# A hybrid attention and GLA layer on one core: the 256-token chunk moved from fifth place to first

## The chip, the cores and the metric

The kernel runs on one core of a Trainium2 chip. The metric is the device time of one launch in microseconds (us), the median of several runs. The engines are TensorE (PE in the profile, PEld for its weight loads), VectorE (DVE), ScalarE (ACT), GpSimd (POOL) and SyncE (SP, which issues most DMAs). Each engine works through its own instructions in order; semaphores make one wait for another.

## What is computed

One layer of a decoder, on 2048 prompt tokens and 64 sample tokens (8 sequences of 8), model width 1024, in float32. Cut to what matters here:

```python
z = jnp.einsum('btd,dn->btn', x, w_in)
q, k, v, g_att, gq, gk, gv, g_gla, g_lr, r_att, r_gla = jnp.split(z, SPLIT_POINTS, axis=-1)
o_att = swa_prompt(q, k, v, attn_sink, rel_table)      # blocks of 128 queries on 256 keys
log_a = jax.nn.log_sigmoid(g_lr @ w_gk_up + b_gk) / 16.
o_gla, S = gla(gq * HK**-0.5, gk, gv, log_a, s0)       # chunked recurrence, state S per head
h_att = (o_att * silu(g_att)) @ w_pa
h_gla = (norm(o_gla) * silu(g_gla)) @ w_pg
merged = sigmoid(r_att) * h_att + sigmoid(r_gla) * h_gla
x = layer_norm(DN_ALPHA * x + merged @ w_o, ln_g, ln_b)
```

The samples go through the same layer with a cache of 128 keys and values and an incoming GLA state. The outputs are the two new x, the last keys and values, and the GLA states.

## The kernel before

**Numbers.** A float32 matrix product is done as three fp32r matmuls: each operand is split into a high part (ACT casts it, line 115) and the rest (line 116, on DVE, in some places on POOL), and high x high, low x high and high x low are summed in PSUM. `proj` (line 176) does this for one output tile: eight slices of 128 inputs, three matmuls each, 24 in all.

**Phases.** Attention (lines 551 to 656), GLA (lines 892 to 972), then the merge of both branches (lines 1115 to 1243) and the output projection with layer norm. Attention and GLA work in chunks of tokens, whose starts and lengths stand in `CHUNKS` (line 42). Attention runs over the chunks once; in each it makes the steps k, v, q0 to q3, a narrow one for the GLA decay (`gl`, lines 637 to 639) and ga0 to ga3. GLA runs over the four heads and in each head over all chunks: one narrow matmul for the decay (`gla_z`, line 686), then v in pieces of 128 tokens (`proj_t`, lines 198 to 200), k, q and two gates. The last chunk, 320 long, is 256 prompt tokens and the 64 samples.

**Weights.** In attention's first chunk each step takes a weight of 512 KB (`wt1`, `wload`): SP loads it into one of two staging buffers (`wst`), ACT casts it, DVE makes the low half (lines 130 to 134). Later chunks use the same ten weights. The first weight comes in four quarters, between the eight pieces of the first chunk's x (lines 229 to 235). During attention's last chunk six GLA weights are loaded, one per step.

**x.** The next chunk's x is fetched in eight pieces and split while the present chunk's gates run (`fetch_x`, `part_x`). There are 20 buffers for 16 parts, so only two pieces can be split ahead; each of the others waits for a slice of the last gate step to be used up.

**Order.** PE's order is the order of the code. Work that hangs on a step's result, such as scores, transposes and outputs, is put in a list of due times, `at(d, fn)`, and one entry is issued after every step (`tick`). A block of 128 queries in attention is issued like this, where `o` is 1 + 3 * bi, 2 more in the first chunk, counted from the last q step:

```python
at(o, lambda A=A, bi=bi: att_scores(A, bi, 0))
at(o + 1, lambda A=A, bi=bi: att_scores(A, bi, 1))
at(o + 3, lambda A=A, bi=bi: att_trans(A, bi, 0))
at(o + 4, lambda A=A, bi=bi: att_trans(A, bi, 1))
at(o + (6 if last and bi else 5), lambda A=A, bi=bi: att_out(A, bi))
```

Five steps follow in the same chunk, so blocks 1 and 2 are finished during the next chunk. `att_scores` (line 367) adds the bias to the scores from PSUM (L384, DVE), takes the maximum (L387, DVE), the exponentials (L390, L392, ACT) and scales (L396, DVE). `att_trans` (line 399) transposes the result on PE (L406) and copies it out as pT, one half on ACT (L410), one on DVE (L408). `att_out` (line 413) multiplies by v (L421) and gates (L424, DVE). In GLA `chain` (line 870) does the same with blocks of the recurrence; a 256-token chunk other than the last has its own due times there (`short`). The samples' state updates (L840) belong to the last chunk and are issued during the next head's first.

The instruction order on ACT, DVE, POOL and SP is set by a scheduler when the kernel is built, from its own estimates. The relative bias table of attention is made during the first chunk (`setup0` to `setup3`): eight tiles in PSUM (L301, L302), copied out by ACT (L306) and DVE (L304). Five PSUM buffers serve all this side work (`pa`), three the steps (`pd`).

Of the kernel before, what the change touches and what calls it, by code (L numbers as in the profile page):

```python
# [38 lines left out]
HV = 256  # L39
CH = 64  # L40

CHUNKS = [(0, 384), (384, 384), (768, 384), (1152, 384), (1536, 256), (1792, 320)]
TM = 384
MT = 352
MS = NT // (2 * MT)
# [6 lines left out]
def kernel(ctx, tc, io):  # L52
# [61 lines left out]
    def split(dst_h, dst_l, src, eng=nc.vector):  # L114
        pin["a"] = nc.scalar.copy(dst_h, src)  # L115
        i = eng.tensor_tensor(dst_l, src, dst_h.bitcast(F32), ALU.subtract)  # L116
        if eng is nc.vector:
            pin["d"] = i
# [5 lines left out]
    def wload(n=1):  # L124
        for _ in range(n):
            i = wseq[0]
            if i >= wseq[1]:
                return
            wseq[0] += 1
            st = sb.tile([P, D], F32, tag="wst", name="wst", bufs=2)  # L130
            pin["w"] = nc.sync.dma_start(st, io["wt"][i])
            hi = wtile(F32R, "wh")
            lo = wtile(F32R, "wl")
            split(hi, lo, st)
            wready.append((hi, lo))
# [12 lines left out]
    def fetch(src, k, t0, T, stage=xstage):  # L148
        st = stage()
        nc.sync.dma_start(st[:, :T], src[:, k, t0:t0 + T])  # L150
        return st, T

    def part(f, new=xnew, eng=nc.vector, samples=False):
        st, T = f
        hi, lo = new(), new()
        split(hi[:, :T], lo[:, :T], st[:, :T], eng)
        if samples:
            nc.gpsimd.tensor_copy(hi[:, T:T + NS], lo[:, T - NS:T])
        return hi, lo
# [4 lines left out]
    def fetch_x(src, t0, T):  # L164

        return [fetch(src, k, t0, T, unit if k < KT // 2 else xstage) for k in range(KT)]
# [63 lines left out]
    for k in range(KT):  # L230
        if k % 2 == 0:
            cs = slice(k * P, (k + 2) * P)
            nc.sync.dma_start(st[:, cs], io["wt"][0, :, cs])
            split(hi[:, cs], lo[:, cs], st[:, cs])
        x.append(part(fetch(io["xT"], k, *CHUNKS[0], unit)))
    wload(2)
# [296 lines left out]
    def wcap(n):  # L533
        wseq[1] = n
# [3 lines left out]
    def gate_in(h, c):  # L538

        t0, T = CHUNKS[c]  # L540
        if c == 0:
# [10 lines left out]
    kprev = vprev = None  # L552
    for c, (t0, T) in enumerate(CHUNKS):
        last = c == len(CHUNKS) - 1
        Tp = T - (NS if last else 0)
# [89 lines left out]
        for g in range(G):  # L645
# [3 lines left out]
            if g == 1:  # L649
                with tc.issue_after(pin["w"].ins) if c == 0 else nullcontext():  # L650
                    xf = fetch_x(io["xT"], *CHUNKS[(c + 1) % len(CHUNKS)])
            if g == G - 2:
# [239 lines left out]
    for h in range(GH):  # L892
        W2 = {}
        wcap(16 + 6 * h)
        for c, (t0, T) in enumerate(CHUNKS):
            last = c == len(CHUNKS) - 1
# [542 lines left out]
```

## Time and profile before

| | us |
|---|---|
| median of 3 runs (lowest, highest) | 1846.34 (1845.18, 1847.78) |
| the profiled execution, its own time | 1846.22 |
| its span | 1844.4 |
| PE busy | 1807.9 |
| DVE busy | 1280.9 |
| ACT busy | 849.9 |
| POOL busy | 422.3 |
| attention, first matmul to the start of GLA | 4.89 to 353.86 |
| GLA, to the last head's last chunk | 353.86 to 1061 |

Times in the rows are counted from the span's start. "Busy" of PE is made of modelled ends of pipelined matmuls, so the distance between the starts of two matmuls says more than the duration of one. "Idle before" names the time in which an engine had nothing to do just before an instruction, and what ended it. The granted clock is 1.00 at 2.4 GHz and 0.50 at 1.2 GHz.

### The profile page before, as it was taken

What the parts mean: (1) busy time and instruction counts of PE and PEld (TensorE: products, weight loads), DVE (VectorE), ACT (ScalarE), POOL (GpSimd) and SP (SyncE); (2) the same over time, 40 slices, a digit from 0 to 9 for tenths busy, and PEclk for the clock granted to TensorE, in tenths of its full rate; (3) what the DMA queues carried; (4) which work ended last, traced back from release to release, by engine and by line L of the source; (5) the groups of instructions that cost most, each with busy time, mean ns of one, the idle gap of its engine ahead of it and who ended that gap; (6) DMA issues with size and microseconds to landing.
All of it is one profiled execution on the core that took longest, in us unless ns stands there. A gap on an engine that the chain in (4) does not pass through costs nothing.

```text
span 1844.4 us, 32399 instructions
## 1 busy us (share of the span) xinstructions
PE 1807.9 (98%) x11683; PEld 1722.2 (93%) x11683; DVE 1280.9 (69%) x2662; ACT 849.9 (46%) x1947; POOL 422.3 (23%) x559
## 2 busy tenths in 40 slices
PE   8999999999999999999999999999999999989997
PEld 7998988899999999999999999999999999988886
DVE  5677778767776776777667669648657566966655
ACT  5444545645665565656546453435443543211110
POOL 3310111300110111011110243430355153631111
PEclk9999999999999999999999999999999999999998
DMA  7211013534345444543543189858887967895531
GB/s 233 63 56 38 12 47 100 165 131 156 120 148 170 143 143 144 186 132 107 181 145 119 58 274 315 283 178 292 276 311 256 310 216 245 287 312 177 166 111 41
DMA packets 199554, 315.84 MB, mean 171 GB/s; under 512 B 21453, under 2 KB 161189, under 8 KB 199376
## 3 DMA queue, kind: packets, MB, share of 16 engines
q1 hardware_dynamic: 192624, 304.61, 50.5%
q0 software_dynamic: 5616, 7.58, 1.5%
q8 instruction: 92, 1.51, 0.3%
q10 hardware_dynamic: 1152, 1.57, 0.3%
q14 instruction: 70, 0.57, 0.1%
HBM read 228.52 MB, written 86.14 MB: 171 GB/s over the span
## 4 chain that ended last, share of the span: by engine, by line
PE 91%; DVE 3%; DMA 3%; issue 1%; POOL 1%; SPq 0%; ACT 0%; DVEq 0%; ACTq 0%; POOLq 0%
PE pd L185 11%; PE pd L187 11%; PE pd L186 11%; PE pa L1234 9%; PE pa L1233 9%; PE pa L1232 9%; PE pd L199 7%; PE pd L198 7%; PE pd L200 7%; PE pa L421 2%; DMA cs<-tt_d 1%; PE pa L406 1%; PE pa L755 1%; PE pa L753 1%; PE pa L754 1%
## 5 line engine op out<-in xcount | busy, mean ns | idle before, releaser
L185 PE MATMUL pd<-x,wh 128*128 128x384 f32 (+2 forms) x1248 | 409.1, 328 | 7.0 <-ACT x L115 6.3
L186 PE MATMUL pd<-x,wh 128*128 128x384 f32 (+2 forms) x1248 | 403.5, 323 | 0.6 <-DVE x L116 0.3
L187 PE MATMUL pd<-x,wl 128*128 128x384 f32 (+2 forms) x1248 | 403.1, 323 | 0.6 <-DVE wl L116 0.6
L1233 PE MATMUL pa<-xl,wh 128*128 128x352 f32 x1176 | 381.3, 324 | 7.9 <-DVE xl L116 7.6
L1232 PE MATMUL pa<-xh,wh 128*128 128x352 f32 x1176 | 381.4, 324 | 2.6 <-ACT xh L115 2.3
L1234 PE MATMUL pa<-xh,wl 128*128 128x352 f32 x1176 | 381.9, 325 | 0.0
L185 PEld LDWEIGHTS pd<-x,wh 128*128 128x128 f32 x1248 | 236.5, 190 | 17.2 <-issue 8.9
L186 PEld LDWEIGHTS pd<-x,wh 128*128 128x128 f32 x1248 | 236.5, 190 | 2.0 <-DVE x L116 1.5
L187 PEld LDWEIGHTS pd<-x,wl 128*128 128x128 f32 x1248 | 236.1, 189 | 1.0 <-DVE wl L116 1.0
L1233 PEld LDWEIGHTS pa<-xl,wh 128*128 128x128 f32 x1176 | 222.7, 189 | 10.4 <-DVE xl L116 10.1
L1232 PEld LDWEIGHTS pa<-xh,wh 128*128 128x128 f32 x1176 | 222.5, 189 | 3.6 <-ACT xh L115 2.6
L1234 PEld LDWEIGHTS pa<-xh,wl 128*128 128x128 f32 x1176 | 224.5, 191 | 0.0
L116 DVE TENSOR_TENSOR xl<-xs,xh 128x1408 fp32r<-128x1408 f32 x63 | 110.5, 1753 | 69.4 <-ACT xh L115 35.7
L198 PE MATMUL pd<-wh,x 128*128 128x256 f32 x512 | 147.9, 289 | 0.0
L199 PE MATMUL pd<-wh,x 128*128 128x256 f32 x512 | 145.6, 284 | 1.2 <-DVE x L116 1.1
L200 PE MATMUL pd<-wl,x 128*128 128x256 f32 x512 | 144.6, 282 | 0.0
L115 ACT CAST x<-xst 128x384 fp32r<-128x384 f32 (+2 forms) x164 | 78.2, 485 | 139.9 <-PE pd L199 117.9
L115 ACT CAST xh<-xs 128x1408 fp32r<-128x1408 f32 x63 | 86.5, 1372 | 103.9 <-PE pa L1234 81.7
L746 POOL TENSOR_SCALAR sq<-sq 128x1 f32<-128x1 f32 (+1 forms) x68 | 21.4, 314 | 467.2 <-ACT ring L745 467.2
L199 PE MATMUL pd<-woh,x 128*128 128x512 f32 x256 | 101.5, 396 | 0.0
L198 PE MATMUL pd<-woh,x 128*128 128x512 f32 x256 | 101.5, 396 | 0.0
L200 PE MATMUL pd<-wol,x 128*128 128x512 f32 x256 | 101.5, 396 | 0.0
(318 smaller groups left out, 3683.6 us busy)
## 6 DMA issues: line engine op xcount, KB each, us to landing
wst<-wt SPq DMA_DIRECT2D x33, 512.0 KB, 3.6
xs<-xc_d SPq DMA_DIRECT2D x24, 704.0 KB, 5.6
cs<-tt_d SPq DMA_DIRECT2D x48, 352.0 KB, 4.7
u<-xT SPq DMA_DIRECT2D x84, 192.0 KB, 4.0
xst<-xT SPq DMA_DIRECT2D x76, 192.0 KB, 2.6
xs<-xT SPq DMA_DIRECT2D x18, 704.0 KB, 5.9
ws<-w_ra SPq DMA_DIRECT2D x36, 256.0 KB, 4.4
ws<-w_rg SPq DMA_DIRECT2D x36, 256.0 KB, 5.6
```

Source lines behind the costliest of these rows:

```text
L115: pin["a"] = nc.scalar.copy(dst_h, src)
L116: i = eng.tensor_tensor(dst_l, src, dst_h.bitcast(F32), ALU.subtract)
L185: mm(ps, hi[:, s], xh[:, :T], start=(k == 0), stop=False)
L186: mm(ps, hi[:, s], xl[:, :T], start=False, stop=False)
L187: mm(ps, lo[:, s], xh[:, :T], start=False, stop=(k == n - 1))
L198: mm(ps, xh[:, xs], hi, start=(k == 0), stop=False)
L199: mm(ps, xl[:, xs], hi, start=False, stop=False)
L200: mm(ps, xh[:, xs], lo, start=False, stop=(k == KT - 1))
L421: mm(ot[pr, :], vb[:, pr], A["pT", bi, kv][:, hf], start=(hf == h0), stop=(hf == 1))
L1232: mm(ps, wh[:, ks], xh[:, ts], start=(k == 0), stop=False)
L1233: mm(ps, wh[:, ks], xl[:, ts], start=False, stop=False)
L1234: mm(ps, wl[:, ks], xh[:, ts], start=False, stop=(k == q.kh - 1))
```

## The change

```diff
-CHUNKS = [(0, 384), (384, 384), (768, 384), (1152, 384), (1536, 256), (1792, 320)]
+CHUNKS = [(0, 256), (256, 384), (640, 384), (1024, 384), (1408, 384), (1792, 320)]
```

The short chunk comes first in attention and in every head of GLA, and the chunk before the last has 384 tokens, three blocks of 128. All loops, due times and buffers stay as they are. What follows from it: in attention's first chunk the ten steps have 256 columns and there are two blocks; in GLA's first chunk of every head there are two v pieces and the `short` due times hold for it; six ticks pass in it, not seven, so that the last entries of the chunk before come a tick later in the second chunk.

The scheduler puts some instructions elsewhere. ACT at the start of the program: `x` and `wh<-wst 128x256` are the first chunk's x and the first weight, `kd` the keys copied out after the k step, `wh<-wst 128x1024` the weights of the next steps, `vT` the copy after the v step. Before:

```order
L115 CAST wh<-wst 128x256
L115 CAST x<-u 128x384 x2
L115 CAST wh<-wst 128x1024
L255 CAST wgs<-wg 128x8x16
L340 CAST kd_231<-pd 64x384
L341 CAST kd_232<-pd 64x384
L115 CAST wh<-wst 128x1024 x2
L345 CAST kd_231<-pd 64x384
```

And now:

```order
L115 CAST wh<-wst 128x256
L115 CAST x<-u 128x256 x2
L340 CAST kd_231<-pd 64x256
L341 CAST kd_232<-pd 64x256
L115 CAST wh<-wst 128x1024
L255 CAST wgs<-wg 128x8x16
L115 CAST wh<-wst 128x1024
L345 CAST kd_231<-pd 64x256
```

The cast of the v step's weight stood ahead of the two copies of the keys and stands behind them now.

DVE in attention's last chunk, from the copies of q0 on: `qa` and `qb` are copies after a q step, `pT` the probabilities turned round, `wl` a GLA weight's low half, `s` scores with the bias, `nm` their maximum. Before:

```order
L363 SCALAR_TENSOR_TENSOR qa<-pd,qa 64x256
L364 SCALAR_TENSOR_TENSOR qb<-pd,qb 64x256
L408 COPY pT<-pa 128x512
L116 TENSOR_TENSOR wl<-wst,wh 128x1024
L363 SCALAR_TENSOR_TENSOR qa<-pd,qa 64x256
L364 SCALAR_TENSOR_TENSOR qb<-pd,qb 64x256
L408 COPY pT<-pa 128x512
L595 COPY vt<-pa 128x256
```

And now:

```order
L363 SCALAR_TENSOR_TENSOR qa<-pd,qa 64x256
L364 SCALAR_TENSOR_TENSOR qb<-pd,qb 64x256
L408 COPY pT<-pa 128x512
L384 TENSOR_TENSOR s<-pa,bias 128x512 x2
L116 TENSOR_TENSOR wl<-wst,wh 128x1024
L387 TENSOR_REDUCE nm<-s 128x4
L388 TENSOR_TENSOR nm<-nm,nsink 128x4
L391 TENSOR_TENSOR es<-sink,nm 128x4
L363 SCALAR_TENSOR_TENSOR qa<-pd,qa 64x256
L364 SCALAR_TENSOR_TENSOR qb<-pd,qb 64x256
L408 COPY pT<-pa 128x512
L595 COPY vt<-pa 128x256
```

The scores of the previous chunk's third block have come in between the copies; a second such group follows after these rows.

## Rows read from the trace of the kernel before

**Rows 1.** The page: the span, and the first line of busy time.

```profile
span 1844.4 us, 32399 instructions
PE 1807.9 (98%) x11683; PEld 1722.2 (93%) x11683; DVE 1280.9 (69%) x2662; ACT 849.9 (46%) x1947; POOL 422.3 (23%) x559
```

**Rows 2.** All waits of PE from 66.4 to 1050 us: what waited, for what, us in total, times, the longest.

```profile
PE pa L421 <- DVE pT L408: 1.1, 1, 1.1
PE pd L199 <- DVE x L116: 1.1, 2, 0.7
PE pd L186 <- POOL x L116: 0.2, 1, 0.2
PE pd L186 <- DVE x L116: 0.2, 1, 0.2
```

**Rows 3.** PE in order of time at the start: start in us, duration, instruction, idle time before it and what ended it. From the top: v (two rows), q0, q1, vT, two of the bias table, q2 (two rows), the second chunk's k.

```profile
14.93 0.44 PE L185 MATMUL pd<-x,wh 128*128 128x384 f32 x1 [0.66 <-ACT wh L115]
...
16.19 0.45 PE L187 MATMUL pd<-x,wl 128*128 128x384 f32 x1 [0.64 <-DVE wl L116]
...
20.14 0.33 PE L185 MATMUL pd<-x,wh 128*128 128x384 f32 x1
...
24.30 0.33 PE L185 MATMUL pd<-x,wh 128*128 128x384 f32 x1
...
28.46 0.49 PE L594 MATMUL pa<-ident,vT 128*128 128x128 f32 x3
...
31.41 0.51 PE L301 MATMUL pa<-oh,rbh 33*128 33x384 f32 x1 [0.84 <-ACT brow L306]
...
35.31 0.69 PE L185 MATMUL pd<-x,wh 128*128 128x384 f32 x1
...
38.36 0.39 PE L185 MATMUL pd<-x,wh 128*128 128x384 f32 x1
...
66.36 0.39 PE L185 MATMUL pd<-x,wh 128*128 128x384 f32 x1
```

**Rows 4.** ACT and DVE in order of time at the start, columns as before: the last two casts of x, the v step's weight, the sixth weight after the first, the first three of DVE's copies of the bias table.

```profile
11.96 1.04 ACT L115 CAST x<-u 128x384 fp32r<-128x384 f32 x2 [0.79 <-DMA u<-xT]
13.83 1.05 ACT L115 CAST wh<-wst 128x1024 fp32r<-128x1024 f32 x1 [0.82 <-DMA wst<-wt]
...
29.87 1.23 DVE L116 TENSOR_TENSOR wl<-wst,wh 128x1024 fp32r<-128x1024 f32 x1 [0.89 <-ACT wh L115]
...
32.76 1.48 DVE L304 COPY brow<-pa 128x384 f32<-128x384 f32 x3
```

**Rows 5.** Busy time by stretch: the stretch and its length, busy time of PE, PEld, DVE, ACT and POOL (instructions), the granted clock, the DMA engines' share, GB/s.

```profile
10.00:12.00 2.00, 2.00 (x10) 1.99 (x9) 1.46 (x3) 0.90 (x4) 0.11 (x1) 1.00 1.00 352
...
32.00:34.00 2.00, 2.00 (x7) 1.50 (x6) 1.97 (x5) 0.64 (x2) 0.00 (x0) 0.50 0.77 238
```

**Rows 6.** The same view by chunk: attention's fifth chunk (256 tokens) and its last.

```profile
252.38:300.31 47.93, 47.93 (x381) 43.29 (x380) 39.51 (x104) 24.68 (x84) 4.23 (x11) 1.00 0.15 48
300.31:353.86 53.55, 52.00 (x352) 46.69 (x350) 39.80 (x90) 28.79 (x81) 16.21 (x33) 1.00 0.49 146
```

**Rows 7.** PE in order of time in attention's fifth chunk: the first matmul of the k step and the first instruction after it.

```profile
252.38 0.28 PE L185 MATMUL pd<-x,wh 128*128 128x256 f32 x1
...
255.27 0.60 PE L406 MATMUL pa<-ident,s 128*128 128x128 f32 x4
```

**Rows 8.** DMA issues by group: what, count, KB each, median us from issue to landing.

```profile
wst<-wt SPq DMA_DIRECT2D x33, 512.0 KB, 3.6
...
u<-xT SPq DMA_DIRECT2D x84, 192.0 KB, 4.0
...
u<-xT SPq DMA_DIRECT2D x20, 128.0 KB, 2.7
```

**Rows 9.** DVE, ACT and PE in order of time in attention's last chunk: two copies of pT and between them the scores of one block and kv head; ACT's exponentials of the same group, first and last; PE's wait in the output of block 0, and the start of the q0 step.

```profile
312.54 0.69 DVE L408 COPY pT<-pa 128x512 f32<-128x512 f32 x1
313.26 1.29 DVE L384 TENSOR_TENSOR s<-pa,bias 128x512 f32<-128x512 f32 x2
314.58 1.22 DVE L387 TENSOR_REDUCE nm<-s 128x4 f32<-128x1024 f32 x1
...
318.71 1.14 DVE L396 TENSOR_SCALAR s<-s,rd 128x256 f32<-128x256 f32 x4
...
322.70 0.69 DVE L408 COPY pT<-pa 128x512 f32<-128x512 f32 x1
...
316.09 0.51 ACT L390 ACTIVATE s<-s,nm 128x256 f32<-128x256 f32 x1 [1.40 <-DVE nm L388]
...
318.08 0.19 ACT L392 ACTIVATE es<-es 128x4 f32<-128x4 f32 x1
...
313.28 1.07 PE L421 MATMUL pa<-pT,vt 128*64 128x512 f32 x2 [1.13 <-DVE pT L408]
314.29 0.41 PE L185 MATMUL pd<-x,wh 128*128 128x320 f32 x1
```

**Rows 10.** DVE and PE in order of time around the second chunk of GLA's second head: three state updates of the samples, the low half of x's last piece, and the matmul that needs it.

```profile
560.01 1.26 DVE L840 SCALAR_TENSOR_TENSOR S<-S,e,pa 128x256 f32<-128x256 f32 x3
...
567.68 0.55 DVE L116 TENSOR_TENSOR x<-xst,x 128x384 fp32r<-128x384 f32 x1
...
569.30 0.28 PE L199 MATMUL pd<-wh,x 128*128 128x256 f32 x1
```

## The prediction

> **What bounds the kernel now.** I read the page first: TensorE (PE) is busy for 98% of the span, VectorE (DVE) for well under that [rows 1]. Busy is not the same as unhindered, so I read next the list of PE's waits, from the second token chunk to the last but one stretch of GLA. In 984 us it holds four lines that add up to 2.6 us [rows 2]: PE runs there without a pause, and no order of the chunks can win more than this. Outside it, the place where a chunk order can win or lose is the start, so I read PE, ACT and DVE in order of time from 0 to 66.36, where the second chunk's first matmul stands [rows 3 to 5]. Last I read what DVE does in each chunk, because a chunk boundary hands attention work of one chunk to the next: 82% in the short chunk and 74% in the last one of attention [rows 6].
>
> The work itself doesn't change. The six lengths are the same six numbers, so matmul columns, blocks, scores, splits and DMA bytes are the same sums. A projection of 24 matmuls takes 4.16 us at 384 columns (20.14 to the next step's start at 24.30, 0.173 each) and 2.89 at 256 (252.38 to 255.27, 0.120 each) [rows 3, 7]. In attention's first chunk ten projections and 16 narrower matmuls get shorter, by 240 x 0.053 + 16 x 0.06 = 13.7 us, and in its fifth chunk they get longer by as much. GLA does likewise four times. What is left is four differences in waiting.
>
> **1. The start of the program.** Eight pieces of x get 64 KB shorter, 0.52 MB in all; at the 352 GB/s that the load ran at between 10 and 12 us [rows 5] that is 1.5 us. The last casts of x, which began at 11.96 [rows 4], begin near 10.5, and with a third off two casts (1.04 us for two) and as much on DVE the k step ends near 12.0. Before, the v weight came at 13.83 and its two halves let PE go on at 14.93 and 16.19 [rows 3, 4]. Now ACT's order puts this weight behind the two k copies that need the k step's end (the first piece of order): about 0.75 us for both, then 1.05 for the cast and 1.22 for DVE's half: 15.1. PE has then idled some 3 us. In the trace a wait of 0.84 us at 31.41, in a stretch of thin matmuls, was followed by a granted clock of 0.50, and the full rate came back at 38.36, 3.05 us after 35.31 [rows 3, 5]; so I count the v step as started at the low clock: 15 matmuls at 0.21 (256 columns at 1.2 GHz), nine at 0.12, end 19.3 against 20.14. q0 and q1 follow at 2.89 each, to 25.1 (before: 28.46, vT).
>
> Then comes the bias table. Its PSUM tiles are emptied by DVE behind the split of the sixth weight, which stood at 29.87, with the copies at 32.76 [rows 4]. Weights come through two staging buffers, each reloaded only after DVE's split; a reload lands after a median of 3.6 us [rows 8], so this chain doesn't shrink with the steps. Worked on from 15.1 it gives the sixth split at 28.5 to 29.7 and the last of the table near 31.5, against 35.31 for q2's start. After that q2 at the low clock for 3.05 us again (4.2), q3 2.9, the gate matmuls 1.9, four projections 11.5 and two rounds of first-block scores 1.7 (16 thin matmuls at some 0.1, an estimate below the 0.12 of 256 columns): the second chunk begins near 53.7 to 53.8. 66.36 - 53.8 = 12.6 is gained where 13.7 is owed: **+1.1 us**. Bounds: -1.5 (the v step keeps the high clock, 1.2, and the chain of weights runs 1.4 ahead of this) and +4.5 (x comes no sooner, 1.5, and the low clock lasts through q3, 24 x 0.09 = 2.2).
>
> The Trainium skill speaks against the first step. Its page "DMA: Bandwidth & Descriptors", section "Anatomy of one DMA — SWDGE (gpsimd) path", gives a transfer a fixed part of about 2 us and 436 GB/s for the rest; by that 64 KB less saves 0.15 us a piece, an estimate, and the start would cost 1.35 us more, 1850.3 in all. The trace's pieces, on another kind of queue, land after a median of 4.0 us at 192 KB and 2.7 at 128 KB [rows 8], which is a third less, not the rule's 4%. I keep the rows' 1.5.
>
> **2. Attention's last chunk.** The chunk ahead of it now has three blocks, not two. Its third block's two score groups and two transposes are therefore issued during the last chunk, in which DVE also splits six GLA weights (the second piece of order). One group costs DVE 1.29 (bias), 1.22 (maximum), 1.14 (scaling) and 0.6 for small ones, 4.3 us, beside 2.2 us in which ACT does its exponentials (316.09 to 318.27) [rows 9]. So 8.6 us and a 0.7 us copy are added to a stretch, v step to gate matmuls, where PE has 24.8 us of work from the q0 step on and DVE's list comes to nearly the same. Walk from q0's start, 314.29: before, DVE reached the copy of block 1's first transposes at 322.70 and ended it 9.1 after that start. Now: two bias adds to 10.4, a weight to 11.6, the maximum to 12.9, exponentials on ACT to 15.2, and behind them on ACT the small sample copy and the pT copy, to 16.1. PE wants that pT for block 1's output at 14.5 (three steps of 320 columns at 0.147 a matmul, halfway between the two pitches, 3.53 each; two rounds of transposes and scores and the vT transposes, 3.9): wait 1.6. Later the second group's probabilities are ready at 23.9, and PE asks at 24.5: no wait. The PSUM tile of the sample rows is released by DVE at 26.7, PE asks at 26.1: 0.6. In all +2.2. The first wait there, 1.13 for pT at 313.28 [rows 9], stays: the same two groups stand ahead of it. The two 0.2 us waits on x at this chunk's head [rows 2] came behind the short chunk and go. **+1.8 us**; bounds -1.5 (also the 1.1 goes, the scheduler's slack holds the rest) and +6 (each of the three inserted DVE pieces comes 1.5 us later than walked).
>
> **3. GLA's first chunk.** PE waited 1.1 us for the low halves of x, twice [rows 2]. These pieces are now a third shorter on DVE and ACT: **-0.6**, between -1.1 and +1 (the chunk itself is shorter, with the samples' attention in it).
>
> **4. The first to the second chunk of each head.** The seventh piece of x was split by 568.23 and needed at 569.30 [rows 10]: 1.07 us to spare. With only two v steps, the state updates of the samples (1.26 us for three) slide by one step, into the x splits. I take 0.1 us per head, **+0.4**, between 0 and +4.
>
> Sum: 1.1 + 1.8 - 0.6 + 0.4 = +2.7 us on the profiled execution's own 1846.22 (span 1844.4), which is the median of before, 1846.34, within 0.12: **1848.9 us**, +0.15%. What measurement can tell from no change is about 0.2%, 3.7 us: below 1842.7 or above 1850.0.
>
> **The rivals.**
> *Nothing but noise (0.20).* DVE's list in the last chunk has slack that I counted as filled, and the start comes out even: 1846.5. For it speaks that a chunk with 82% on DVE ran without a wait of PE [rows 6]; against it that the staging chain doesn't get shorter.
> *The last chunk becomes DVE's (0.22): slower.* Place: from q0 to the sample rows of attention's last chunk. DVE is in order, and each of ACT's exponentials puts 2.2 us between its pieces. With 8.6 + 0.7 us more, DVE has 49 us in about 58 (53.55 and some 5 of PE's own), 84% against 74%, and all of the addition falls into the chunk's first half; it decides from the point where a pT copy comes later than 16.1 in the walk above, since every following piece then comes later too. At +6 there and +3 at the start, with the other two at 0: 1855.
> *The shorter first load wins (0.08): faster.* If PE gets going with 128 KB pieces at a time and no low clock follows, 2.7 us less at the start, and the 2.6 us of [rows 2] go while the last chunk adds nothing: 1846.2 - 1.5 - 2.6 = 1842. Against it speaks that the v weight, not x, is what PE waits for at 14.93 and 16.19.
>
> **How the numbers follow.** My forecast has 0.50, with its own range of 1847 to 1851. It lies inside the 0.2% band for four fifths: same 0.40, slower 0.10. The first rival adds 0.20 to same, the second 0.22 to slower, the third is split 0.06 faster and 0.02 same. That gives faster 0.06, same 0.62, slower 0.32. For 8 in 10 the range takes in half of the slow rival and the near side of the fast one: 1845 to 1854.
>
> **What will show it.** Second chunk's first matmul near 53.8 (start right), an idle of 2 to 3 us before the v step's low half, PEclk low once more before 20 us. In attention's last chunk DVE near 84% and new PE waits for pT or a PSUM tile that add up to about 2 us; no wait for x at its head. The waits for x at GLA's head at or below 1.1. Wrong would be: PE waits over 3 us in the list between the second chunk and the end of GLA outside that chunk, or a start that differs from 53.8 by more than 3.

## The result: 0.44% slower

The changed kernel took 1854.62 us (median of 7 runs, 1851.37 to 1858.70), the kernel before 1846.65 (7 runs, 1845.18 to 1848.54): ratio 1.0044, 95% interval 1.0031 to 1.0057, some 8 us. The forecast was 1848.9 in a range of 1845 to 1854. The profiled execution took 1852.60 us, 6.4 more than the one of before.

The page after, its span and busy line, beside [rows 1]:

```profile
span 1850.8 us, 32403 instructions
PE 1812.3 (98%) x11683; PEld 1725.4 (93%) x11683; DVE 1271.4 (69%) x2662; ACT 848.7 (46%) x1947; POOL 426.7 (23%) x559
```

The shares are the same; 6.4 us don't show in them. All waits of PE after the first chunk, from 56.9 to 1050 us, in the columns of [rows 2]:

```profile
PE pa L753 <- ACT st L115: 3.7, 3, 1.2
PE pa L421 <- DVE pT L408: 0.6, 1, 0.6
```

All x waits of [rows 2] are gone, the wait for pT halved, and a line stands there that no step of the prediction had: the matmul of GLA's state, three times 1.2 us. Then the start, PE in the columns of [rows 3]:

```profile
14.82 0.58 PE L185 MATMUL pd<-x,wh 128*128 128x256 f32 x1 [1.90 <-ACT wh L115]
...
16.32 0.58 PE L187 MATMUL pd<-x,wl 128*128 128x256 f32 x1 [0.71 <-DVE wl L116]
...
20.97 0.41 PE L187 MATMUL pd<-x,wl 128*128 128x256 f32 x1
21.18 0.31 PE L185 MATMUL pd<-x,wh 128*128 128x256 f32 x1
...
30.79 0.44 PE L301 MATMUL pa<-oh,rbh 33*128 33x384 f32 x1 [1.80 <-DVE vt L595]
...
34.01 0.58 PE L185 MATMUL pd<-x,wh 128*128 128x256 f32 x1
...
38.02 0.41 PE L185 MATMUL pd<-x,wh 128*128 128x256 f32 x1
38.23 0.32 PE L186 MATMUL pd<-x,wh 128*128 128x256 f32 x1
...
56.84 0.39 PE L185 MATMUL pd<-x,wh 128*128 128x384 f32 x1
```

The second chunk begins at 56.84, not near 53.8. From 16.70 on the matmuls of the v step start 0.21 us apart, up to 21.18, where q0 begins, and those of q2 up to 38.23. For 256 columns this is the pitch of 1.2 GHz (256 / 1.2 = 213 ns); it is called the low pitch below, beside the 0.120 of [rows 7]. Why the v step began late stands on ACT and DVE, to be read beside [rows 4]:

```profile
12.95 0.36 ACT L340 CAST kd<-pd 64x256 fp32r<-64x256 f32 x1 [2.00 <-PE pd L187]
13.33 0.37 ACT L341 CAST kd<-pd 64x256 fp32r<-64x256 f32 x1
13.72 1.04 ACT L115 CAST wh<-wst 128x1024 fp32r<-128x1024 f32 x1
...
14.60 0.42 DVE L343 TENSOR_TENSOR kl<-pd,kd 64x256 fp32r<-64x256 f32 x1
15.04 1.23 DVE L116 TENSOR_TENSOR wl<-wst,wh 128x1024 fp32r<-128x1024 f32 x1
```

ACT idles two microseconds for the k step, copies keys, and only then casts the v weight, whose load (issued at 6.42) had landed after 5.5 us, at 11.9. DVE's half of it comes behind copies of keys as well.

Where the 6.4 us are, by the starts of PE's chunks in both profiled executions (us). "Owed" is what a chunk of 256 tokens takes less than one of 384: 61.98, attention's fifth chunk after, less the 47.93 of [rows 6].

| stretch | before | after | difference |
|---|---|---|---|
| attention's first chunk ends (owed: 14.05 less) | 66.36 | 56.84 | +4.5 |
| the rest of attention (owed: 14.05 more) | 287.50 | 301.16 | -0.4 |
| GLA heads 0, 1, 2 | 178.72, 172.45, 172.44 | 178.80, 174.12, 174.10 | +0.1, +1.7, +1.7 |
| GLA head 3, to the first matmul of the merge | 184.22 | 183.38 | -0.8 |
| merge and output | 782.7 | 782.4 | -0.3 |

Head 0 has the state's wait too, but lost its x waits. What the state waits for is seen on DVE and ACT in head 0's last chunk, with PE's matmul below:

```profile
518.47 1.23 DVE L116 TENSOR_TENSOR wl<-wst,wh 128x1024 fp32r<-128x1024 f32 x1 [0.49 <-ACT wh L115]
519.61 0.41 DVE L926 TENSOR_TENSOR vs<-vs,pd 64x256 f32<-64x256 f32 x1
519.94 1.21 DVE L116 TENSOR_TENSOR wl<-wst,wh 128x1024 fp32r<-128x1024 f32 x1
521.08 0.47 DVE L771 SCALAR_TENSOR_TENSOR ring<-ring,e,pa 128x256 f32<-128x256 f32 x1
...
521.92 0.47 ACT L748 ACTIVATE ring<-pa,sq 128x256 f32<-128x256 f32 x1 [1.63 <-POOL sq L747]
522.29 0.39 ACT L115 CAST x<-u 128x256 fp32r<-128x256 f32 x1
522.58 0.40 ACT L115 CAST st<-ring 128x256 fp32r<-128x256 f32 x1
...
523.04 0.38 PE L753 MATMUL pa<-st,qih 128*128 128x256 f32 x1 [1.24 <-ACT st L115]
```

The state after the first block (L771) was ready to be made from PSUM at about 517.6, but DVE first split two weights of the next head. The state's cast then stood on ACT behind two other instructions, a microsecond after the end of L771. PE reached the next block's matmul at 521.6 and waited for that cast: 1.4 us by the starts, and the two matmuls behind it came 0.49 and 0.22 us apart instead of 0.12, together some 1.8 us. The chunk ahead now has three blocks, whose state steps follow each other after one step; the old short chunk's stood two steps apart, `(3, 5)`.

### The profile page after: what moved, and what is told of

Read it like the earlier page. It is cut to its first block, busy times and chain, and to the rows that moved or that the text cites. A ratio compares the mean times of both kernels' runs of the same rounds, so it can differ in the third digit from the quotient of the medians.

```text
span 1850.8 us, 32403 instructions
## 1 busy us (share of the span) xinstructions
PE 1812.3 (98%) x11683; PEld 1725.4 (93%) x11683; DVE 1271.4 (69%) x2662; ACT 848.7 (46%) x1947; POOL 426.7 (23%) x559
## 4 chain that ended last, share of the span: by engine, by line
PE 87%; DVE 4%; DMA 3%; ACT 2%; issue 2%; POOL 1%; SPq 0%; DVEq 0%; ACTq 0%; POOLq 0%
PE pd L185 10%; PE pd L187 10%; PE pd L186 10%; PE pa L1233 9%; PE pa L1232 9%; PE pa L1234 9%; PE pd L199 6%; PE pd L200 6%; PE pd L198 6%; DMA cs<-tt_d 2%; PE pa L421 1%; PE pa L406 1%; PE pa L754 1%; PE pa L755 1%; PE pa L753 1%
## 5 line engine op out<-in xcount | busy, mean ns | idle before, releaser
L1233 PEld LDWEIGHTS pa<-xl,wh 128*128 128x128 f32 x1176 | 223.5, 190 | 10.5 <-DVE xl L116 10.5
```

The source lines that it names most:

```text
L1233: mm(ps, wh[:, ks], xl[:, ts], start=False, stop=False)
```

## Experiments

Starts of the second chunk and of the merge are the first matmul there in each profiled execution. Ratios are to the kernel before, timed on the same chip.

**E1 and E2: the new order in one phase alone.**

```diff
+GCHUNKS = ...
-        for c, (t0, T) in enumerate(CHUNKS):
+        for c, (t0, T) in enumerate(GCHUNKS):
```

(the loop over GLA's chunks, its fetches and `gate_in`; attention's last fetch takes GLA's first chunk)

> The new order in attention alone, GLA keeps the old one. The changed kernel's trace has the second chunk's first matmul at 56.84, 4.5 us later than 66.36 less the 14.05 that chunk 5 takes longer; attention ends at 358.00 against 353.86. Theory (two places: the start and the last chunk of GLA's first three heads): here only the start is left, attention ends at 358.0, the three waits of L753 (3.7 us) are absent, the two waits for x at GLA's head (1.1 us) are back: own time 1846.2 + 4.1 = 1850.3. Rival (all of the loss lies in GLA): attention ends within 1 us of 353.9, own time 1846.

> The new order in GLA alone, attention keeps the old one. Theory: attention ends at 353.9, the three waits of L753 in the last chunk of heads 0 to 2 are there with 1.2 us each and some 1.75 us of lost time each (5.3), the two waits for x at GLA's head go (-1.4 us), the last head ends 0.9 earlier: +2.6, own time 1848.8. Rival (the loss is the start alone): GLA ends no later than before, own time 1845 to 1846.

E1: attention ended at 357.63, no L753 wait in heads 0 to 2, x waits 0.2 instead of 1.1; merge at 1064.35, 2.7 after the kernel before. E2: attention ended at 352.00, with three L753 waits again (four with the last head, 4.3 us); GLA to the merge 710.5 us against 707.8. So both places exist, each without the other. Up to the merge this is as expected, but for the x waits, which should have been back in E1 with GLA's old order. The totals were not: ratios 1.0043 [1.0028, 1.0057] and 1.0052 [1.0032, 1.0072]. Their merges took 588.8 and 587.2 us from first to last matmul, where before and after take 582.5 and 581.7; in E2, 4.0 of it is one wait, taken up in E6.

**E3: later weights in GLA's last chunk.**

```diff
-                if last and i < 2:
-                    wload()
...
-            if len(CHUNKS) - 4 < c < len(CHUNKS) - 1:
+            if c > len(CHUNKS) - 4:
                 wload()
...
             gla_q(B, ps[:, :T])
+            if last:
+                wload()
```

> The changed kernel, with the two weights of the next head in GLA's last chunk loaded and split at the k and the q step and not at the first two v steps. Theory (the state update L771 of the first of three blocks stands behind two weight splits of 1.22 us on DVE): L771 follows its matmuls within 0.5 us, the three L753 waits fall below 0.3 us each, GLA gets 5.3 us shorter, own time 1852.6 - 5.3 = 1847.3. Rival (the chain from one block's state to the next is too long for the one k step between them, whatever else DVE does): the waits stay above 1 us each, own time 1852 to 1853.

DVE and ACT in the same place as above:

```profile
519.47 0.47 DVE L771 SCALAR_TENSOR_TENSOR ring<-ring,e,pa 128x256 f32<-128x256 f32 x1
...
522.31 1.23 DVE L116 TENSOR_TENSOR wl<-wst,wh 128x1024 fp32r<-128x1024 f32 x1 [0.78 <-ACT wh L115]
...
520.43 0.41 ACT L115 CAST st<-ring 128x256 fp32r<-128x256 f32 x1
...
522.85 0.28 PE L753 MATMUL pa<-st,qih 128*128 128x256 f32 x1
```

The state goes first, its cast ends two microseconds ahead of PE, and heads 0 to 2 have no wait left. Heads 0 to 2 took 176.96, 172.31 and 172.26: 5.5 us less than in the changed kernel, where 5.3 was expected. One k step is long enough for the state's chain; the weights were the cause. The ratio fell to 1.0024 [1.0010, 1.0039], some 3.7 us; this interval and that of the changed kernel still overlap a little. The profiled execution itself (1853.50) shows no gain: its start was 1.2 later and its merge took 585.4.

**E4: the v weight ahead of the key copies.**

```diff
+            if c == 0:
+                with tc.issue_after(pv["a"].ins), tc.issue_after(pv["d"].ins):
+                    att_keys(A, ps[:, :Tp], Tp)
```

(`pv`: the v weight's cast and split)

> The changed kernel, with the copies of the first chunk's keys held behind the v weight's cast (ACT) and split (DVE), which is the order of the kernel before. Theory (the v weight, landed at 11.9, waits 1.8 us on ACT for the key copies, and the delay goes on to the next weights and the bias table): v's first matmul near 13.0 and not 14.82, v's low half near 14.3 and not 16.32, the second chunk's first matmul 1.5 to 2 us earlier, at 55.0; own time 1850.8. If the shorter pause also spares the doubled pitch of the v step (0.213 us a matmul and not 0.120) another 2.2: 1848.6. Rival (the chain of weights through two staging buffers sets the start anyway): q2 starts at 34.0 as now, own time 1852.6.

```profile
13.03 0.58 PE L185 MATMUL pd<-x,wh 128*128 128x256 f32 x1 [0.33 <-ACT wh L115]
14.29 0.39 PE L187 MATMUL pd<-x,wl 128*128 128x256 f32 x1 [0.47 <-DVE wl L116]
...
28.27 0.68 PE L303 MATMUL pa<-oh,rbh 33*128 33x384 f32 x1 [1.55 <-DVE vt L601]
...
32.06 0.58 PE L185 MATMUL pd<-x,wh 128*128 128x256 f32 x1
...
55.50 0.39 PE L185 MATMUL pd<-x,wh 128*128 128x384 f32 x1
```

v began at the times expected, its matmuls came 0.12 us apart, and q0 began at 17.02 instead of 21.18. But of these 4.2 us only 1.3 reached the second chunk (55.50): the bias table came earlier too and waited again. In the times it doesn't show: 1.0043 [1.0029, 1.0057].

**E5: the table one step later.**

```diff
-            at(1, setup1)
-            at(2, setup2)
+            at(2, setup1)
+            at(3, setup2)
```

> The changed kernel, with the bias table's matmuls (and the loads that follow them) issued one step later, after q2 and not after q1. In the changed kernel PE pauses 1.80 us in the table, for the copy of vt, and q2 behind it runs at the doubled pitch (24 x 0.213). Theory (the shorter steps bring the table before DVE can empty its tiles, and pause and low clock are the loss): q2 runs at 27.2 with 0.120 a matmul, the table has a pause below 0.5 us, q3 starts near 33.3, the second chunk between 51.3 and 54.3 (56.84 to 58.00 without the move), own time 1847 to 1850. Rival (the weights through two staging buffers set the start): q3 and ga0 wait for their weights instead, and the second chunk still starts at 56 or later.

PE in the table, and ACT ahead of it:

```profile
35.34 0.69 PE L301 MATMUL pa<-oh,rbh 33*128 33x384 f32 x1 [3.46 <-ACT brow L306]
...
33.74 1.04 ACT L115 CAST wh<-wst 128x1024 fp32r<-128x1024 f32 x1 [2.70 <-DMA wst<-wt]
34.81 1.24 ACT L306 COPY brow<-pa 128x384 f32<-128x384 f32 x3
```

The theory fell: the pause grew from 1.80 to 3.46, second chunk at 58.08, ratio 1.0055 [1.0036, 1.0073]. The copy that PE wanted stood on ACT behind the cast of a weight that was still on its way.

**E6 and E7: old order in attention, new one in GLA, with E3's weights; E7 with E5's table too.** The diffs are those of E2 and E3, for E7 of E5 as well.

> Attention in the old order, GLA in the new one, and the two weights of GLA's last chunk at the k and q step. Theory (in GLA the new order costs only the L753 waits, which the later weights remove, and it spares the two waits for x at the head): GLA starts as before, 352.0 to 353.9, no wait of PE above 0.3 us in GLA, first matmul of the merge 2.9 us ahead of the kernel before (1061.69) for the same start of GLA: 1058.8 less what the start brings. Own time 1843.3 or, with the faster of the two starts seen, 1841.5. Rival (the later weights hold up something else in the next head): head 1 to 3 begin with waits for weights, no gain over before.

> The kernel of the run before (old order in attention, new one in GLA, later weights), and the bias table one step later. Theory (in the old order too the pause in the table, 0.64 to 0.84 us, and at times a low clock behind it, are lost time): q2 at 28.7 with 0.173 a matmul, no pause in the table, second chunk between 60.9 and 62.5 (66.36 and 64.50 so far), own time 1839 to 1841. Rival (in the old order the table is hidden well enough, its pause only moves to the next weight): second chunk at 64 to 66, own time as the run before.

Up to the merge both came out about as expected: E6 began it at 1059.12 (1058.8 forecast) with no wait over 0.6 us in GLA up to 1058, E7 had its second chunk at 61.71 and the merge at 1054.17, 7.5 us ahead of the kernel before. Yet the ratios were 1.0015 [1.0002, 1.0028] and 1.0009 [0.9997, 1.0022]. The longest of E6's waits of PE from 1059 to 1066, and DVE there:

```profile
PE pa L1235 <- DVE wl L117: 4.3, 1, 4.3
```

```profile
1060.04 0.88 DVE L117 TENSOR_TENSOR xl<-xc,xh 128x704 fp32r<-128x704 f32 x1
1065.20 1.10 DVE L117 TENSOR_TENSOR wl<-ws,wh 128x256 fp32r<-128x256 f32 x3 [4.29 <-DMA ug_d<-sg]
```

The merge's first weight is written where GLA's last gate still lies, and waits for that gate's store to leave. The chunk orders themselves aren't the reason; which of the rotating buffers the last gates got is, as E11 shows.

**E8 to E10: the changed kernel with more help at the start.** E8 has the edits of E3, E4 and E5; E9 is the changed kernel with two more staging buffers; E10 is E8 with these two.

```diff
-            st = sb.tile([P, D], F32, tag="wst", name="wst", bufs=2)
+            st = stile("wst2") if i in (2, 3) else sb.tile(...)
...
-    wload(2)
+    wload(4)
```

> The changed kernel (new order in both) with all three edits: later weights in GLA's last chunk, the v weight's cast ahead of the key copies, the table one step later. Theory: second chunk between 50 and 53, GLA starts at 351 to 354, no wait above 0.6 us up to GLA's end, merge begins near 1057 to 1059, own time 1841 to 1844. If the short chunk first is worse in itself (work of the first chunk that doesn't shrink with its tokens, ten weights through two buffers): second chunk at 54 or later, 1846 or more.

> The changed kernel, with the weights of q0 and q1 staged in two buffers of their own (those that the bias takes later), so that four weights and not two are on their way from the start. Theory (the ten weights of the first chunk come through two buffers at 3 to 4 us each, longer than a step of 256 columns, 2.9, and this supply bounds the start): the weights of q2 and later are cast 3 us or more earlier, the pause in the bias table gets below 1 us, the second chunk starts between 52 and 55 (56.4 to 58.0 in three runs with the new order in attention); median 2 to 5 us below that of the changed kernel, own time 1848 to 1851. Rival (it is ACT's and DVE's own order and load, not the supply): the pause stays near 1.8 us and the second chunk at 56 or later.

> The run with all three edits on the changed kernel, and the two additional staging buffers. In that run the first copy of the table stood on ACT behind the cast of the next weight, which waited 1.92 us for its DMA, and PE paused 3.63 us. Theory of supply: that wait is gone, pause in the table below 1 us, second chunk between 49.5 and 52.5 (55.79 without), GLA from 351 to 354, merge begins at 1056 to 1059, median 3 to 5 us below the run without, near 1844 to 1846. Rival: the pause stays above 2.5 us and the second chunk above 55.

All three missed. Second chunk at 55.79, 59.06 and 59.92; pauses in the table of 3.63 (E8), 1.20 and 0.91 with another 0.99 ahead of it (E9), 1.13 with 2.80 (E10); ratios 1.0017 [1.0004, 1.0030], 1.0075 [1.0059, 1.0090] and 1.0044 [1.0029, 1.0059]. E8's gain over the changed kernel is about E3's. In E9 the weights did come earlier (the sixth cast at 24.86, not 29.50), but the table's own inputs are pinned behind the newest weight (`issue_after` in `setup0`) and came later with it. So E9 and E10 are no clean test of the supply. E12 to E14 leave the loads, casts and splits of six weights out together: they test the weights' work as a whole, and don't tell the loads from the rest.

**E11: E7 with one small buffer taken ahead of the last gates.**

```diff
+                if last and h == GH - 1 and m == 0:
+                    nc.gpsimd.memset(unit(name="pad")[:, :1], 0.0)
                 sg = unit(name="sg")
```

> Old order in attention, new one in GLA, later weights, table one step later, and one small buffer more taken ahead of the last head's last gates, so that these lie in other buffers. In the three kernels that mixed the orders the merge begins with a wait of 4.0 to 5.0 us of PE for the low half of the first weight, which DVE can write only when the store of the last gate has left that memory. Theory: this wait is an accident of the buffers; it goes, the merge takes 582 to 583 us and not 586.7, second chunk near 61.7, merge begins near 1055, own time 1838 to 1840, median 4 to 5 us below the run before and clearly below the kernel before (ratio near 0.997). Rival (the merge takes its time whatever it begins with): the merge takes 586 to 588, no change of the median.

The waits of PE from 1057 to 1066 are now:

```profile
PE pa L1236 <- DVE xl L117: 1.4, 1, 1.4
PE pa L1235 <- ACT wh L116: 0.3, 1, 0.3
```

The 4.3 us are gone, the merge took 581.5 us. Median 1841.82 against 1846.30 for the kernel before on that chip: ratio 0.9978 [0.9967, 0.9989], the only version that beats both kernels. Its second chunk began at 65.02, though, as without the later table; E7's 61.71 was not seen again, so how much the table's place gives in the old order stays open. Most of the difference is the clock: behind the table the granted clock fell to 0.50 in E11 and stayed at 1.00 in E7, and q3 with the narrow step took 9.49 us against 7.07.

**E12 to E15: leaving work out of the first chunk** (one profiled execution each).

```diff
+            if 4 <= i < 10:
+                wready.append(W0[i % 2])
+                continue
```

(E12 in the changed kernel, E13 in the kernel before, E14 with E4's edit as well; E15 has E4's edit, all weights, and no table matmuls)

> The changed kernel without six of the ten weights of the first chunk: q2, q3 and the gates use those of k and v again, so six loads, casts and splits are left out and PE's work stays. Theory (fixed work: the casts and splits of ten weights, which don't get shorter with the chunk, and ACT's and DVE's order around them, hold up what PE wants of ACT and DVE at the table): no pause in the table above 0.5 us, q2 at 30.3 and not 34.01, second chunk at 50.9; the loss at the v step (3.6 us against the kernel before) stays. Rival (the table by itself is too early in the short chunk): pause near 1.8 us and second chunk at 54 or later.

> The kernel before with the same six weights left out. Theory: table without a pause, q2 at 31.4 to 31.7 with 0.173 a matmul, second chunk at 60.7 (66.36, 64.50 and 65.79 in the three runs with this order and all weights); less 14.05, what the short chunk owes, this is 46.65, against which the two other runs are held. Rival: as with all weights, 64.5 to 66.4.

> The changed kernel with the v weight's cast ahead of the key copies and the same six weights left out. Theory (two causes, one after the other: the v weight's place on ACT, then the fixed work of the other weights): q0 at 17.0, table without a pause near 24, second chunk at 47.7, that is within 1 to 1.5 us of the old order's time less 14.05. Rival (only one of the two counts): no better than the run without the v edit, 50.9.

> The changed kernel with the v weight's cast ahead, all ten weights, and without the bias table's eight pairs of matmuls and their copies (the table is zeros). Theory (the weights' fixed work holds PE up wherever it next asks ACT or DVE for something): PE waits at q2, q3 or the first gate for a weight, 2 us or more in all, second chunk at 48.5 or later though 3 us of matmuls are gone. Rival (the table alone is the cause): no such wait, q2 at 24.3, second chunk at 44.9 to 46.

The second chunk's first matmul in E12, E13, E14 and E15, in this order:

```profile
54.12 0.39 PE L190 MATMUL pd<-x,wh 128*128 128x384 f32 x1
```

```profile
64.79 0.39 PE L190 MATMUL pd<-x,wh 128*128 128x384 f32 x1
```

```profile
51.97 0.39 PE L190 MATMUL pd<-x,wh 128*128 128x384 f32 x1
```

```profile
49.21 0.39 PE L185 MATMUL pd<-x,wh 128*128 128x384 f32 x1
```

The pause in the table was gone in E12, E13 and E14. The forecasts of these three were 3 to 4 us too early, in part because the low pitch behind the table stayed: q2 still took 4.48 us in E12 and 6.59 in E13. In E14 the v step had it too, so that q0 began at 19.28, where E4 and E8 had 17.02 and 16.99. The differences say more. With all weights, the new order's second chunk began at 56.84, 56.42 and 58.00 in three kernels that leave attention as it is, the old one's at 66.36, 64.50 and 65.79: means 57.09 and 65.55, a loss of 57.09 - (65.55 - 14.05) = 5.6 us. Without the six weights it is 54.12 - (64.79 - 14.05) = 3.4, and with the v weight ahead too, 51.97 - 50.74 = 1.2. So some 2.2 us of the loss are the weights' work that doesn't shrink with the chunk, some 2.2 the v weight's place, and 1.2 is left, less than the 2 us (22 x 0.093) that the low pitch of the v step still cost in E14. Starts of one kind lie up to 1.9 us apart and E12 to E14 are one execution each, so each share is good to one or two microseconds. In E15 PE waited three times for a weight's low half, 1.7 us in all (2 or more expected), and the start stood at 49.21 where the table alone as a cause would have given 45 to 46: without the table, the weights hold PE up elsewhere. Some 1.8 us of that gap, though, are the v step, at the low pitch here too (q0 at 18.82).

## Why the prediction was wrong

**The start (+1.1 forecast, +4.5 in the profiled execution, +5.6 by the means).** The mechanism was right, the sizes were not. The load did get shorter: the last x casts began at 10.24 (10.5 forecast, 11.96 before). Over all traces they began at 9.71 to 10.75 with the short chunk first and at 10.95 to 11.96 otherwise, in the mean 1.1 us apart. That is less than the rows' 1.5. The 0.15 us estimated from the Trainium skill's page "DMA: Bandwidth & Descriptors", section "Anatomy of one DMA — SWDGE (gpsimd) path", was too little; the page gives its figures for transfers issued by GpSimd, and these are issued by SyncE. v's first matmul came at 14.82, but its low half at 16.32 and not 15.1: the k step, whose last matmuls came at the low pitch as well, ended at 12.9 and not near 12.0, and three key copies on DVE, which the step left out, held the split back from 14.76 to 15.04. The low pitch lasted for the whole v step and not for 15 matmuls: v ended at 21.18, not 19.3. (The v step has it in nine of the eleven traces with the short chunk first, all but E4 and E8, and in none of the six others.) Then the weights: the third was cast at 21.68, behind the copy of v on ACT, though it had landed at 19.79, and the sixth split ran from 30.65 to 31.87, where 28.5 to 29.7 was forecast. The table paused for 1.80 us and q2 began at 34.01, not near 31.5. The bound of +4.5 was in the text (its terms, 1.1 + 1.5 + 2.2, come to 4.8); the value taken inside it was too hopeful, since it let a chain of ten weights run on while every link waited in order behind a step's copies.

**Attention's last chunk (+1.8 forecast, -0.4 measured for all of attention behind the first chunk).** The chunk took 5.4 us more with the third block's work (58.92 against 53.55), and the second chunk, which now receives two blocks and not three, 5.8 less. The wait at block 1's output was there. PE's rows, after and then before:

```profile
326.22 3.06 PE L421 MATMUL pa<-pT,vt 128*64 128x512 f32 x8
329.21 0.41 PE L185 MATMUL pd<-x,wh 128*128 128x320 f32 x1
```

```profile
327.01 1.94 PE L421 MATMUL pa<-pT,vt 128*64 128x512 f32 x8
328.87 0.42 PE L185 MATMUL pd<-x,wh 128*128 128x320 f32 x1
```

Eight matmuls take 1.1 us longer (1.6 forecast), though the list of waits has no line for it: the stall lies inside the group, up to the end of pT's copy on ACT at 327.30. The first pT wait halved (0.57 for 1.13), where the step had it stay, and the two x waits went. The step for the sample rows (0.6) can't be told apart in these rows. DVE was busy for 81% of the chunk (84% forecast), in the columns of [rows 6]:

```profile
299.08:358.00 58.92, 58.30 (x392) 50.89 (x390) 47.87 (x115) 33.21 (x101) 15.49 (x34) 1.00 0.35 109
```

The slow rival, with this chunk as its place, named 1855. The time came out there by luck: its place did not, and nothing of the loss is here.

**GLA's first chunk (-0.6 forecast).** Both x waits went, near its bound of -1.1. That the shorter pieces are the reason isn't shown: E1 and E13, with GLA's old order, had only 0.2 and 0.3 us of them left.

**The first to the second chunk of each head (+0.4).** Small, as forecast: PE's list has no wait there.

**What was missing.** No step looked at GLA's chunk before the last, which grows from two blocks to three and loses its own due times; the prediction put this at nothing. It followed the short chunk to its new place in every head, but not what took its old one. That is +5.5 us in heads 0 to 2, which E3 takes away. Against it, head 0 gave back 1.8, the x waits among it, heads 1 and 2 gave back 0.3, and the last head 0.8, where the state's own waits went from 1.1 to 0.6: net +2.6. With the start's +4.5, attention's -0.4 and the merge's -0.3 these are the 6.4 us of the profiled pair. With a start of +5.6, by the means, it is +7.8 up to the merge, beside 8.0 of the medians; but the merge alone differs by more than this between executions, so that agreement proves little. Both things that the prediction had named as showing it wrong came: waits of 3.7 us in GLA, and a start 3.04 us from 53.8.

## What to carry to other kernels

A shorter first chunk shortens PE's work and the loads of tokens, but not that of the weights: count what doesn't shrink, and look on each in-order engine for what PE wants next standing behind a cast that waits for its load. When pieces change places, go through both places, the one that the short piece left too, and there look at each chain whose links now follow one step closer. And read whole phases behind an edit: E6 and E7 were 2.6 and 7.5 us ahead at the merge and lost 4.3 and 5.0 us there to a buffer.

## What was not expected

PE's pitch and the granted clock don't always agree. In the v step after, 256 columns took 0.213 us, the rate of 1.2 GHz, while the clock's column reads 1.00; in the table it reads 0.50:

```profile
16.00:18.00 2.00, 1.68 (x8) 1.68 (x9) 1.99 (x5) 0.00 (x0) 0.00 (x0) 1.00 0.35 68
32.00:34.00 2.00, 2.00 (x8) 1.56 (x6) 1.73 (x4) 0.81 (x2) 0.00 (x0) 0.50 0.81 215
```

In E3 and E5 the same step, at the same pitch, reads 0.50 from 18 to 20 us, so here the pitch says more than the column. Ahead of the first stretch PE had been busy for 0.91 and 0.80 of two microseconds each.

The low pitch behind the table needs no pause: in E12 and E13 PE ran through the table without a wait and q2 began slow all the same. Nor does the table always bring it: of the 16 traces with the table, E7, without a wait there either, is the one whose next step ran at full rate. In E15, without the table, q2 took 2.97 us, full rate. What decides between E7 and the others stays open.

The merge took between 577.9 (E13) and 588.8 us (E1) in the profiled executions, with the same matmuls. A part of this is pace: 1680 matmuls in a row, from the merge's 673rd on and without a wait, took 266.9 us in the changed kernel, 268.8 in the one before and 270.7 in E1 and E8. Apart from that and from the 4 to 5 us of the buffer in E2, E6 and E7, the differences aren't explained, so the medians of E1, E4 and E5 can't be held against their starts to better than a few microseconds.
